# Reciprocal roots by logarithm and exponential, and a ring of four places for the block operands, in a one-core Hymba layer

## The chip, the cores and the metric

The kernel runs on one core of a Trainium2 chip. The metric is the device time in microseconds (us) of one execution. A core has five engines that run their own instruction queues in order: PE (TensorE: matrix products and transposes), DVE (VectorE), ACT (ScalarE: functions from loaded tables, copies with a scale), POOL (GpSimd, used here mostly to issue stores) and SP (SyncE, which issues loads). They meet through semaphores.

## The reference

One layer of a hybrid decoder on a prompt of 1024 tokens and on eight sequences of one new token each, model width 1024, all in fp32:

```python
hn = rmsnorm(x, g_norm)
u = hn @ w_in                                  # one input projection, 1024 x 7176
xa, za, uq, uk, uv, uo, zb, ui, uf = jnp.split(u, SPLIT_IDX, axis=-1)
yA = rglru_branch(xa, ...)                     # conv of 4, gates, linear recurrence
h, C, n, m = mlstm_seq(q, k, v, ig, lf, ...)   # 4 heads of 256, chunks of 128 tokens
yB = jax.nn.sigmoid(uo) * hB
yB = yB * lax.rsqrt(jnp.mean(yB * yB, axis=-1, keepdims=True) + EPS)   # one norm per token and head
merged = concat[yA * silu(za), yB * g_mhead * silu(zb)]
x = x + merged @ w_out                         # 2048 -> 1024
y = x * lax.rsqrt(jnp.mean(x * x, axis=-1, keepdims=True) + EPS) * g_final
```

It returns y for the prompt and for the new tokens, and the states of both branches.

## The kernel before

Every fp32 product is made of three matmuls on operands that are split into a rounded high part (a copy by ACT, `split`, L72) and the remainder (a subtraction by DVE, L73); in the groups of the profile they are L66, L67 and L68 of `mm3`. Large products are done in blocks by a scheme with seven products instead of eight.

The first 650 us or so make the input projection, the RG-LRU branch and the decode step of the mLSTM. What the change touches lies behind that. There the loop over n = 4..31 goes through 8 chunks of 128 tokens and, in each, 4 heads. For each n it emits the work of one head: `m_k` (weights `We` by an exponential on ACT, the split of q into `qh`, `ql` and of the state into `Ch`, `Cl`), `m_a` (scores in `ps_s`, keys `kh`, `kl`, weighted scores `ph`, `pl`, values `vh`, `vl`), `m_b` (products with the state in `ps_qp`, keys by values in `ps_kv`, scores by values in `ps_tr`, the new state `Cf`, the head's output `hh`) and `m_g` (gate by `so`, sum of squares by a Square on ACT). At the start of the next chunk `m_n` takes the reciprocal root for the four heads of the chunk before, a tile `ms` of 128x4; `m_zg` multiplies the four `hh` by it on ACT, and `m_z` transposes them on PE (into `ps_s` for the first two heads, `ps_qp` for the others) and multiplies by `z`. The root is `rsqrt`: a Sqrt on ACT, a reciprocal on DVE, a correction in one step (128x1) or two (128x4), and another reciprocal. The function needs a table, which ACT loads by an instruction of its own (ACT_TABLE_LOAD); where Sqrt follows an exponential or the reverse, a load stands ahead of it.

Between these pieces `fill` puts pieces of the output projection. For the first two thirds they are the 28 products `r_prod` of the seven-product scheme, over blocks whose operands `r_op` splits from raw blocks in DRAM (`d_ro`). The raw blocks come through a ring of SBUF places: two tiles of four (`ring0`, `ring1`), so that `r_op(n)` fetches block n + 8 into the place it has just split. `ring1` takes a slot (number 5) that an earlier weight operand held, and is opened in `r_prod(1)`; the same slot later holds z's block `zb0`, which is read back from DRAM. After the products come `out_part` pieces for the rows of tokens that go through the plain scheme, tile by tile (`wo` with `mh`, `ml`), each ending in an add on DVE (`y`, L1562) and a Square on ACT (L1563), and in `finish`, which takes a reciprocal root of a 128x1 tile `fms` and scales y for its store. `last_tile` does the same for the last 128 tokens with its own root (a tile `ms` of 128x1), and ends the kernel with two scalings (`yg`, L1593 on DVE and L1594 on ACT) and two stores.

The code emits instructions in this order; a scheduler in the framework then sets the order of each engine's queue, except where a stretch is put in by hand for PE. So another function or another count of operations can also move what stands around it.

Of the kernel before, what the change touches and what calls it, by code (L numbers as in the profile page):

```python
# [9 lines left out]
F32 = mybir.dt.float32  # L10
F32R = mybir.dt.float32r
BF16 = mybir.dt.bfloat16
AF = mybir.ActivationFunctionType
ALU = mybir.AluOpType
# [3 lines left out]
P = 128  # L18
T = 1024
HT = 512  # L20
# [31 lines left out]
def hymba_kernel(  # L52
# [7 lines left out]
    V, A, G, TE = nc.vector, nc.scalar, nc.gpsimd, nc.tensor  # L60
# [28 lines left out]
    rawp = ctx.enter_context(tc.tile_pool(name="rawp", bufs=1))  # L89
# [96 lines left out]
    def rsqrt_mean(out, v, t, n):  # L186

        V.tensor_scalar(v, v, 0.25 / n, 0.25 * EPS, op0=ALU.mult, op1=ALU.add)
        rsqrt(out, v, t)

    def rsqrt(out, v, t):

        A.activation(out, v, AF.Sqrt)
        V.reciprocal(t, out)
        if len(v.shape) == 2 and v.shape[1] == 1:
            V.scalar_tensor_tensor(t, v, t, out, op0=ALU.mult, op1=ALU.add)
        else:
            V.tensor_tensor(t, t, v, op=ALU.mult)
            V.tensor_tensor(t, t, out, op=ALU.add)
        V.reciprocal(out, t)  # L200
# [36 lines left out]
    def dec_unit(u):  # L237

        pz = ps("tr", [P, 512])
        for k in range(KC):  # L240
            g = k % 4
            TE.matmul(pz[32 * g:32 * g + 32, :], hnd[:, NB * k:NB * k + 32], raws[u, k // 4][:, k % 4, :], start=k < 4, stop=k >= 4,  # L242
                      skip_group_check=True)
        Z = sg([P, 512], "Z")
        A.copy(Z, pz)

        def turn():
            pt = ps("tr", [P, 4, P])
            for m in range(4):
                TE.transpose(pt[:, m, :], Z[:, m * P:(m + 1) * P], idF)  # L250
            for a, (kind, j) in enumerate(units[u]):
                src = pt[:, 2 * a:2 * a + 2].rearrange("p m (g b) -> p m b g", g=4)[:, :, 0:NB, :]
                V.tensor_reduce(dec_dst[kind](j), src, axis=mybir.AxisListType.X, op=ALU.add)
                if kind == "k":
                    V.tensor_scalar(dec_dst[kind](j), dec_dst[kind](j), 1.0 / 16.0, None, op0=ALU.mult)
        late.append(turn)
# [4 lines left out]
    def blk(u, a, b):  # L261
        return raws[u, b][:, :, a * 256:(a + 1) * 256]

    def prep(u, q):
        if q == Q_P5:
            dec_unit(u)
            V.tensor_tensor(blk(u, 0, 0), blk(u, 0, 0), blk(u, 1, 0), op=ALU.subtract)
            V.tensor_tensor(blk(u, 1, 0), blk(u, 1, 0), blk(u, 1, 1), op=ALU.add)
        if q == Q_P6:
            V.tensor_tensor(blk(u, 1, 0), blk(u, 1, 1), blk(u, 0, 0), op=ALU.subtract)  # L270
        src = {Q_P1: (0, 0), Q_P2: (0, 1), Q_P5: (1, 0), Q_P6: (1, 0), Q_P7: (0, 0), Q_P3: (0, 1), Q_P4: (1, 1)}
        hi, lo = ws([P, 4, 256], f"wh{u}_{q}"), ws([P, 4, 256], f"wl{u}_{q}")
        split(hi, lo, blk(u, *src[q]))
        wops[u, q] = hi, lo
        if q == Q_P6:
            V.tensor_tensor(blk(u, 0, 1), blk(u, 0, 1), blk(u, 1, 0), op=ALU.subtract)
        b = {Q_P7: 0, Q_P4: 1}.get(q)
        if b is not None:
            if u + 1 < len(units):
                load_raw(u + 1, b)  # L280
            else:
                if b == 1:
                    r_open(0)

    px = {}

# [976 lines left out]
    def m_n(c):  # L1263

        m = ch[c]["m"]
        dn, ss, t, rs, u = (m[:, n] for n in range(5))
        V.scalar_tensor_tensor(t, dn, -1.0, em_t[:, c, :], op0=ALU.mult, op1=ALU.max)
        V.tensor_tensor(t, t, dn, op=ALU.max)
        V.scalar_tensor_tensor(t, t, 0.25 * EPS, t, op0=ALU.mult, op1=ALU.mult)
        V.scalar_tensor_tensor(t, ss, 0.25 / (4 * 256), t, op0=ALU.mult, op1=ALU.add)  # L1270
        rsqrt(rs, t, u)

    def m_zg(c):

# [54 lines left out]
    def slot(n, name, dt=F32R):  # L1329
        if n < 0:  # L1330
            return rawp.tile([P, 4, HT], dt, tag="raw0", name=name)
        return big(n, [P, 4, HT], name, dt)
# [53 lines left out]
    rring = []  # L1386
    rops = {}
    rx = {}

    def r_open(n):  # L1390

        rring.append(rawp.tile([P, 4, HT], F32, tag="raw1", name="ring0") if n == 0 else slot(5, "ring1", F32))
        for i in range(4):
            r_fetch(4 * n + i)

    def r_slot(n):
        return rring[n % 8 // 4][:, n % 4, :]

    def r_fetch(n):

        if n < NR:
            p, q = n // 7, RQ[n % 7]
            ld(r_slot(n), d_ro[q][:, p].rearrange("p k t -> p (k t)"))

    def r_op(n):

        if n < NR:
            rops[n] = o = ws([P, 2, HT], f"ro{n}")
            split(o[:, 0], o[:, 1], r_slot(n))
            r_fetch(n + 8)  # L1410

    def put(c, a, t):
        stq(d_p[c][a], t, accum_op=ALU.add)
# [1 line left out]
    def r_prod(n):  # L1415

        p, q = n // 7, RQ[n % 7]
        if n < 2:
            w_step((Q_P4, Q_P3)[n])
        if n == 1:  # L1420
            r_open(1)
        r_op(n + 2)
        o = rops.pop(n)
        oh, ol = (o[:, i].rearrange("p (k t) -> p k t", k=4) for i in range(2))
        wh, wl = wr[q]
        if q == Q_P1:
            rx["X"] = ps("o", [P, 512])
        if q in (Q_P2, Q_P5):
            rx["Y"] = ps("o", [P, 512])
        X, Y = rx["X"], rx.get("Y")  # L1430
        out = X if q in (Q_P1, Q_P6, Q_P7, Q_P4) else Y
        for k in range(4):
            mm3(out, oh[:, k, :], ol[:, k, :], wh[:, k, :], wl[:, k, :], q in (Q_P1, Q_P2, Q_P5) and k == 0,
                q in (Q_P2, Q_P4, Q_P3) and k == 3)
            if k % 2:
                yield
        c = 4 * (p // 2) + p % 2
        if q in (Q_P1, Q_P5, Q_P6, Q_P4):
            rx[q] = t = sg([P, HT], f"r{q}")
            A.copy(t, Y if q == Q_P5 else X)  # L1440
            if q == Q_P4:
                put(c, 1, t)
        else:
            t = rx.pop({Q_P2: Q_P1, Q_P7: Q_P5, Q_P3: Q_P6}[q])
            V.tensor_tensor(t, t, X if q == Q_P7 else Y, op=ALU.add)
            put(c if q == Q_P2 else c + 2, q == Q_P7, t)
        r_after(n - (NR - 7))
# [59 lines left out]
    def finish(n, yt, ms, dst, later=False):  # L1507

        V.tensor_scalar(ms[:n, 0:1], ms[:n, 0:1], ms[:n, 1:2], 0.25 / T, op0=ALU.add, op1=ALU.mult)
        V.tensor_scalar(ms[:n, 0:1], ms[:n, 0:1], 0.25 * EPS, None, op0=ALU.add)  # L1510
        rsqrt(ms[:n, 2:3], ms[:n, 0:1], ms[:n, 3:4])

        def out():
            for half in range(2):
                hs = slice(half * HT, (half + 1) * HT)
                V.scalar_tensor_tensor(yt[half][:n], yt[half][:n], ms[:n, 2:3], mx["gf"][half][:n], op0=ALU.mult, op1=ALU.mult)
                stq(dst[:, hs], yt[half][:n])
        if later:
            tails.append(out)
        else:  # L1520
            out()
# [49 lines left out]
    def last_tile():  # L1571
        ms = mx["p2"].tile([P, 6], F32, tag="ms7", name="ms7")
        y = [sg([P, HT], f"y{n}") for n in range(2)]
        yg = [sg([P, HT], f"yg{n}") for n in range(2)]
        for n in range(2):
            ld(y[n], d_p[NCH - 1][n])
        mh, ml = ch[NCH - 1]["mh"], ch[NCH - 1]["ml"]
        for i, cs in enumerate(LP):
            p = ps("o", [P, 512])[:, 0:cs.stop - cs.start]
            for k in range(8):  # L1580
                w = wo[8 + k]
                mm3(p, mh[:, k, :], ml[:, k, :], w[:, 0, cs], w[:, 1, cs], k == 0, k == 7)
            v = (y[0], y[1][:, 0:256], y[1][:, 256:512])[i]
            vg = (yg[0], yg[1][:, 0:256], yg[1][:, 256:512])[i]
            gv = (mx["gf"][0], mx["gf"][1][:, 0:256], mx["gf"][1][:, 256:512])[i]
            V.tensor_tensor(v, v, p, op=ALU.add)
            A.activation(p, v, AF.Square, accum_out=ms[:, i:i + 1])
            V.tensor_tensor(vg, v, gv, op=ALU.mult)
            if i == 1:
                V.tensor_scalar(ms[:, 0:1], ms[:, 0:1], ms[:, 1:2], T * EPS, op0=ALU.add, op1=ALU.add)  # L1590
        V.tensor_scalar(ms[:, 0:1], ms[:, 0:1], ms[:, 2:3], 0.25 / T, op0=ALU.add, op1=ALU.mult)
        rsqrt(ms[:, 4:5], ms[:, 0:1], ms[:, 5:6])
        V.tensor_scalar(yg[0], yg[0], ms[:, 4:5], None, op0=ALU.mult)  # L1593
        A.mul(yg[1], yg[1], ms[:, 4:5])  # L1594
        for n in range(2):
            ld(y_p[0, (NCH - 1) * P:T, n * HT:(n + 1) * HT], yg[n])
# [152 lines left out]
    while work:  # L1749
        fill(1)  # L1750
    tail()
    last_tile()
    es_m.close()

# [32 lines left out]
```

## Time and profile before

| | us |
|---|---|
| time, median of 3 runs | 923.3 |
| lowest, highest | 921.3, 925.6 |
| the profiled execution | 925.6 |
| its span | 923.8 |
| PE busy | 905.8 (98%) |
| DVE busy | 742.0 (80%) |
| ACT busy | 613.6 (66%) |
| POOL busy | 192.7 (21%) |

A line of the timeline gives the start in us from the span's start, the duration, the engine, the line of the kernel, the operation, what it writes and reads by the names of the program, and in brackets the idle time ahead of it with what ended it. A line of waits gives total, times and longest. A line of a group gives busy time and the mean of one instruction in ns. Some 1.8 us of the execution lie outside of its span.

### The profile page before, as it was taken

The numbers are of one execution on the slowest core, as the hardware profiler recorded it, in microseconds if no ns is written. First come the engines' busy times: TensorE is split into PE (matmuls) and PEld (weight loads), VectorE is DVE, ScalarE is ACT, GpSimd is POOL, SyncE is SP. The second block draws the span as 40 slices with busy tenths as digits, with TensorE's granted clock in tenths as the row PEclk, the third lists the DMA queues.
The fourth block names the chain that finished last, engine by engine and source line by source line (L and its number), as shares of the span: only waits on it lengthen the run. The fifth ranks groups of instructions, "written<-read, shape, count | busy, mean of one in ns | idle before, by whom it ended". The sixth has DMA issues, their size and how long they took to land.

```text
span 923.8 us, 15540 instructions
## 1 busy us (share of the span) xinstructions
PE 905.8 (98%) x5261; PEld 749.8 (81%) x5261; DVE 742.0 (80%) x1535; ACT 613.6 (66%) x1088; POOL 192.7 (21%) x317
## 2 busy tenths in 40 slices
PE   8999999999999999999999999999999999999997
PEld 6798777777787988787789898877778888878886
DVE  6776778978688878789888876679997779888874
ACT  7654446866667776576758775446878579687772
POOL 1111113112312222324332324010111111110120
PEclk9999999999999999999999999999999999999999
DMA  6611457365746566547665647336588879755753
GB/s 195 212 46 40 143 151 251 127 207 176 239 141 205 171 202 195 187 145 260 210 232 168 252 137 241 107 131 220 181 241 242 212 209 294 189 163 149 197 106 94
DMA packets 130600, 167.87 MB, mean 182 GB/s; under 512 B 17620, under 2 KB 98580, under 8 KB 130514
## 3 DMA queue, kind: packets, MB, share of 16 engines
q1 hardware_dynamic: 108938, 103.94, 37.4%
q0 software_dynamic: 21584, 62.95, 20.7%
q8 instruction: 41, 0.67, 0.3%
q14 instruction: 37, 0.30, 0.1%
HBM read 108.19 MB, written 62.92 MB: 185 GB/s over the span
## 4 chain that ended last, share of the span: by engine, by line
PE 82%; DMA 6%; ACT 4%; DVE 4%; issue 2%; SPq 0%; POOL 0%; ACTq 0%; DVEq 0%; POOLq 0%
PE ps_o L66 14%; PE ps_o L68 13%; PE ps_o L67 13%; PE ps_kv L66 10%; PE ps_kv L67 9%; PE ps_kv L68 9%; PE ps_tr L242 2%; DMA Cb<-in_state_mlstm_C_dram 2%; PE ps_s L1181 1%; PE ps_qp L67 1%; DMA x<-in_x_prompt_dram 1%; PE ps_qp L68 1%; PE ps_qp L66 1%; PE ps_qp L999 1%; PE ps_tr L250 1%
## 5 line engine op out<-in xcount | busy, mean ns | idle before, releaser
L72 ACT CAST wh<-raw 128x1024 fp32r<-128x1024 f32 x91 | 95.4, 1049 | 76.3 <-PE ps_o L67 24.3
L73 DVE TENSOR_TENSOR wl<-raw,wh 128x1024 fp32r<-128x1024 f32 x91 | 111.1, 1220 | 31.2 <-ACT wh L72 17.9
L66 PE MATMUL ps_kv<-cb_hi,wh 128*128 128x512 f32 x320 | 127.5, 398 | 0.0
L68 PE MATMUL ps_kv<-cb_hi,wl 128*128 128x512 f32 x320 | 125.3, 392 | 0.0
L67 PE MATMUL ps_kv<-cb_lo,wh 128*128 128x512 f32 x320 | 125.2, 391 | 0.0
L66 PE MATMUL ps_o<-cb_hi,wh 128*128 128x512 f32 x240 | 94.6, 394 | 0.0
L68 PE MATMUL ps_o<-cb_hi,wl 128*128 128x512 f32 x240 | 93.6, 390 | 0.0
L67 PE MATMUL ps_o<-cb_lo,wh 128*128 128x512 f32 x240 | 93.5, 390 | 0.0
L66 PEld LDWEIGHTS ps_kv<-cb_hi,wh 128*128 128x128 f32 x320 | 60.1, 188 | 21.4 <-issue 4.6
L67 PEld LDWEIGHTS ps_kv<-cb_lo,wh 128*128 128x128 f32 x320 | 60.2, 188 | 13.4 <-issue 1.7
L68 PEld LDWEIGHTS ps_kv<-cb_hi,wl 128*128 128x128 f32 x320 | 60.1, 188 | 12.9
L66 PE MATMUL ps_kv<-wh,cb_hi 128*128 128x256 f32 x192 | 55.3, 288 | 0.3 <-ACT s L326 0.3
L67 PE MATMUL ps_kv<-wl,cb_hi 128*128 128x256 f32 x192 | 54.4, 283 | 0.0
L68 PE MATMUL ps_kv<-wh,cb_lo 128*128 128x256 f32 x192 | 54.3, 283 | 0.0
L66 PE MATMUL ps_o<-wo,mh 128*128 128x512 f32 (+1 forms) x136 | 53.2, 391 | 0.0
L66 PEld LDWEIGHTS ps_o<-cb_hi,wh 128*128 128x128 f32 x240 | 45.1, 188 | 9.9 <-issue 0.8
L68 PEld LDWEIGHTS ps_o<-cb_hi,wl 128*128 128x128 f32 x240 | 45.1, 188 | 9.8
L67 PEld LDWEIGHTS ps_o<-cb_lo,wh 128*128 128x128 f32 x240 | 45.1, 188 | 9.1
L68 PE MATMUL ps_o<-wo,ml 128*128 128x512 f32 (+1 forms) x136 | 51.8, 381 | 0.0
L67 PE MATMUL ps_o<-wo,mh 128*128 128x512 f32 (+1 forms) x136 | 51.4, 378 | 0.0
L66 PE MATMUL ps_o<-wh,cb_hi 128*128 128x256 f32 x144 | 40.9, 284 | 0.0
L67 PE MATMUL ps_o<-wl,cb_hi 128*128 128x256 f32 x144 | 40.7, 283 | 0.0
(545 smaller groups left out, 2624.5 us busy)
## 6 DMA issues: line engine op xcount, KB each, us to landing
raw<-in_w_in_dram SPq DMA_DIRECT2D x55, 512.0 KB
Cb<-in_state_mlstm_C_dram SPq DMA_DIRECT2D x32, 256.0 KB
out_dram<-Cb POOLq DMA_DIRECT2D x32, 256.0 KB, 4.4
qk<-d_qk SPq DMA_DIRECT2D x32, 256.0 KB
ring<-d_ro SPq DMA_DIRECT2D x28, 256.0 KB
d_qk<-s POOLq DMA_DIRECT2D x24, 256.0 KB, 4.4
d_x<-s POOLq DMA_DIRECT2D x16, 256.0 KB, 3.2
zsr<-d_y SPq DMA_DIRECT2D x16, 256.0 KB
```

The costliest lines, as they stand in the source:

```text
L66: TE.matmul(out, ah, bh, start=first, stop=False, skip_group_check=True)
L67: TE.matmul(out, ah, bl, start=False, stop=False, skip_group_check=True)
L68: TE.matmul(out, al, bh, start=False, stop=last, skip_group_check=True)
L72: A.copy(hi, src)
L73: V.tensor_tensor(lo, src, hi.bitcast(F32), op=ALU.subtract)
L242: TE.matmul(pz[32 * g:32 * g + 32, :], hnd[:, NB * k:NB * k + 32], raws[u, k // 4][:, k % 4, :], start=k < 4, stop=k >= 4, skip_group_chec ...
L250: TE.transpose(pt[:, m, :], Z[:, m * P:(m + 1) * P], idF)
L999: TE.matmul(pq[32 * g:32 * g + n, 0:256], q, ds_["C", h * NB + bb][:, kb, :], start=b == 1, stop=b == NB - 1, skip_group_check=True)
L1181: TE.matmul(S, qk[:, 2 + kb, :], qk[:, kb, :], start=kb == 0, stop=kb == 1)
```

## The change

A new function takes the reciprocal root as exp(-ln(v) / 2), with one Newton step on DVE. It replaces `rsqrt` in `m_n` (8 times, 128x4), in `finish` (8 times, 128x1 and once 8x1) and in `last_tile` (once, 128x1). The norm of the input, and other roots earlier, keep `rsqrt`. And the raw blocks' ring has one tile of four places; `r_op(n)` fetches block n + 4 into the place it has split, `ring1` is gone, and slot 5 goes straight to `zb0`. From the new function on, the lines stand 12 further down (10 from `r_prod` on).

```diff
+    def rsqrt_log(out, v, t):
+
+        A.activation(t, v, AF.Ln)
+        A.activation(out, t, AF.Exp, scale=-0.5)
+        if len(v.shape) == 2 and v.shape[1] == 1:
+            V.scalar_tensor_tensor(t, out, out, v, op0=ALU.mult, op1=ALU.mult)
+        else:
+            V.tensor_tensor(t, out, out, op=ALU.mult)
+            V.tensor_tensor(t, t, v, op=ALU.mult)
+        V.tensor_scalar(t, t, -0.25, 0.75, op0=ALU.mult, op1=ALU.add)
+        V.tensor_tensor(out, out, t, op=ALU.mult)
...
                 if b == 1:
-                    r_open(0)
+                    r_open()
...
     def m_n(c):
...
-        rsqrt(rs, t, u)
+        rsqrt_log(rs, t, u)
...
-    def r_open(n):
-
-        rring.append(rawp.tile([P, 4, HT], F32, tag="raw1", name="ring0") if n == 0 else slot(5, "ring1", F32))
+    def r_open():
+
+        rring.append(rawp.tile([P, 4, HT], F32, tag="raw1", name="ring"))
         for i in range(4):
-            r_fetch(4 * n + i)
+            r_fetch(i)
 
     def r_slot(n):
-        return rring[n % 8 // 4][:, n % 4, :]
+        return rring[0][:, n % 4, :]
...
             split(o[:, 0], o[:, 1], r_slot(n))
-            r_fetch(n + 8)
+            r_fetch(n + 4)
...
     def r_prod(n):
...
-        if n == 1:
-            r_open(1)
...
     def finish(n, yt, ms, dst, later=False):
...
-        rsqrt(ms[:n, 2:3], ms[:n, 0:1], ms[:n, 3:4])
+        rsqrt_log(ms[:n, 2:3], ms[:n, 0:1], ms[:n, 3:4])
...
     def last_tile():
...
-        rsqrt(ms[:, 4:5], ms[:, 0:1], ms[:, 5:6])
+        rsqrt_log(ms[:, 4:5], ms[:, 0:1], ms[:, 5:6])
```

In the built programs ACT has 61 table loads before and 70 now. Three places of the order, first ACT around `m_n(5)`, from the root's load to the gate of the next head. Before:

```order
L193 ACT_TABLE_LOAD
L193 ACTIVATE ms<-ms 128x4
L72 COPY qh<-qk 128x256
L72 COPY Ch<-Cf_5975 128x516
L1237 ACTIVATE hh<-ps_qp,gi_t 128x257
L193 ACTIVATE fms<-fms 128x1
L1189 ACTIVATE kh<-ps_s,de_t 128x256
L72 COPY vh<-vt 128x256
L193 ACTIVATE fms<-fms 8x1
L1277 ACTIVATE hh<-hh,ms 128x256
L72 COPY ph<-pf 128x128
L1277 ACTIVATE hh<-hh,ms 128x256 x3
```

Now, ahead of which stand a first load, the Ln of `ms` and the Ln of the decode step's 8x1 `fms` (L193):

```order
L194 ACT_TABLE_LOAD
L194 ACTIVATE ms<-ms 128x4
L194 ACTIVATE fms<-fms 8x1
L72 COPY qh<-qk 128x256
L72 COPY Ch<-Cf_5975 128x516
L1249 ACTIVATE hh<-ps_qp,gi_t 128x257
L1573 ACTIVATE ps_o,fms<-y_9122 128x512
L72 COPY vh<-vt 128x256
```

and directly behind these:

```order
L1289 ACTIVATE hh<-hh,ms 128x256 x3
L1201 ACTIVATE kh<-ps_s,de_t 128x256
L193 ACT_TABLE_LOAD
L193 ACTIVATE fms<-fms 128x1
L1272 ACTIVATE so,ms<-hh 128x256
L194 ACT_TABLE_LOAD
L194 ACTIVATE fms<-fms 128x1
L72 COPY ph<-pf 128x128
L1289 ACTIVATE hh<-hh,ms 128x256
```

`kh` moved from the third place behind the state's copy to behind a Square and three `hh`, and `ph` behind two more loads and the gate's Square.

The second place is ACT around `m_n(6)`. Before, from the load for `We`:

```order
L1162 ACT_TABLE_LOAD
L1162 ACTIVATE We<-We 128x128
L193 ACT_TABLE_LOAD
L193 ACTIVATE ms<-ms 128x4
L72 COPY qh<-qk 128x256
L72 COPY Ch<-Cf_5975 128x516
L1563 ACTIVATE ps_o,fms<-y_9629 128x512
L1237 ACTIVATE hh<-ps_qp,gi_t 128x257
L1189 ACTIVATE kh<-ps_s,de_t 128x256
```

Now:

```order
L1174 ACTIVATE We<-We 128x128
L1573 ACTIVATE ps_o,fms<-y_9640 128x512
L193 ACT_TABLE_LOAD
L193 ACTIVATE ms<-ms 128x4
L72 COPY qh<-qk 128x256
L194 ACT_TABLE_LOAD
L194 ACTIVATE ms<-ms 128x4
L72 COPY Ch<-Cf_5975 128x516
L1249 ACTIVATE hh<-ps_qp,gi_t 128x257
L72 COPY vh<-vt 128x256
L1289 ACTIVATE hh<-hh,ms 128x256 x2
L1201 ACTIVATE kh<-ps_s,de_t 128x256
```

`We` has lost its load, the Exp's load stands ahead of `Ch`, and two `hh` ahead of `kh`. On PE the transposes of `hh` into `ps_s` moved ahead of the `Ch` products of this piece.

The third place is the end of the loop, the root of the last chunk and of one output tile. ACT before:

```order
L1563 ACTIVATE ps_o,fms<-y_9870 128x512
L193 ACT_TABLE_LOAD
L193 ACTIVATE ms<-ms 128x4
L193 ACTIVATE fms<-fms 128x1
L1277 ACTIVATE hh<-hh,ms 128x256 x4
```

ACT now:

```order
L1573 ACTIVATE ps_o,fms<-y_9882 128x512
L193 ACT_TABLE_LOAD
L193 ACTIVATE ms<-ms 128x4
L194 ACT_TABLE_LOAD
L194 ACTIVATE ms<-ms 128x4
L193 ACT_TABLE_LOAD
L193 ACTIVATE fms<-fms 128x1
L194 ACT_TABLE_LOAD
L194 ACTIVATE fms<-fms 128x1
L1289 ACTIVATE hh<-hh,ms 128x256 x4
```

Four loads stand ahead of the four `hh` where one did. On PE the four transposes of `hh` into `ps_s` stand two matmuls further ahead. In what follows, the next output tile's `fms` and the last tile's `ms` have two loads each, where before they had none.

## Prediction

> **What bounds the kernel now.** I read the page first, then the waits of PE in the second half, then the instructions at each place where a root is taken. The page's busy row and the chain that ended last:
>
> ```profile
> PE 905.8 (98%) x5261; PEld 749.8 (81%) x5261; DVE 742.0 (80%) x1535; ACT 613.6 (66%) x1088; POOL 192.7 (21%) x317
> ...
> PE 82%; DMA 6%; ACT 4%; DVE 4%; issue 2%; SPq 0%; POOL 0%; ACTq 0%; DVEq 0%; POOLq 0%
> ```
>
> PE is the bound, and it stands still hardly at all. Its waits from 600 us to the end, of which three lines matter here:
>
> ```profile
> PE ps_qp L1286 <- ACT hh L1237: 1.2, 1, 1.2
> ...
> PE ps_s L1286 <- ACT hh L1277: 0.7, 1, 0.7
> PE ps_o L66 <- ACT ro L72: 0.4, 1, 0.4
> ```
>
> So a PE that runs full has next to nothing to win: what the change can give is in these lines, and what it can cost is every microsecond by which an operand now comes after PE asks for it. The roots are ACT's. The line of the root (the tile `ms` of m_n and of the last tile), with the loads of ScalarE's tables (min/median/max in ns), and the loads ahead of We's exponential:
>
> ```profile
> L193 ACT ACT_TABLE_LOAD  x13: 1283/1283/1283, 631.5 to 895.3; - x13
> L193 ACT ACTIVATE ms<-ms x9: 203/206/208, 632.8 to 918.5; 128x4 f32<-128x4 f32 x8, 128x1 f32<-128x1 f32 x1
> ...
> L1162 ACT ACT_TABLE_LOAD x11 | 14.1, 1283 | 0.2
> ```
>
> A load is 1.28 us and the root 0.2 us: the load is the price.
>
> **The change: arithmetic.** On DVE each root keeps its count: reciprocal, one or two steps, reciprocal become three or four steps of the same sizes, so the work there costs nothing. What changes is ACT. In the order of the changed program every Ln has a load ahead of it, and every Exp as well. In the stretch of m_n the second load replaces the one ahead of We, so their number stays, but both now stand ahead of the root's consumers, and what is queued behind them on ACT (qh, Ch, hh, kh, ph) is what PE asks for. I price the places one after another.
>
> **The last tile.** The end of before on ACT, and DVE's step ahead of the root:
>
> ```profile
> 917.99 0.19 ACT L1587 ACTIVATION_READ_ACCUMULATOR ps_o<-y 128x1 f32 x1
> 918.46 0.20 ACT L193 ACTIVATE ms<-ms 128x1 f32<-128x1 f32 x1 [0.28 <-DVE ms L1591]
> 919.35 0.72 ACT L1594 ACTIVATE yg<-yg,ms 128x512 f32<-128x512 f32 x1 [0.68 <-DVE ms L200]
> ...
> 918.21 0.21 DVE L1591 TENSOR_SCALAR ms<-ms 128x1 f32<-128x1 f32 x1 [0.18 <-ACT ps_o L1587]
> ```
>
> No load is left here before. Now the Ln's load starts at 918.18, when the accumulator is read, and hides only DVE's step: Ln 919.47 to 919.67, the Exp's load to 920.95, Exp to 921.15, against a root that ended at 918.66. DVE's steps behind it keep their 0.69 (918.66 to 919.35). This is the chain that ends the kernel: **+2.5**.
>
> **m_n of the last chunk.** ACT, then PE:
>
> ```profile
> 895.10 0.19 ACT L1563 ACTIVATION_READ_ACCUMULATOR ps_o<-y 128x1 f32 x1
> 895.31 1.28 ACT L193 ACT_TABLE_LOAD   x1
> 896.60 0.21 ACT L193 ACTIVATE ms<-ms 128x4 f32<-128x4 f32 x1
> 897.67 1.71 ACT L1277 ACTIVATE hh<-hh,ms 128x256 f32<-128x256 f32 x4 [0.77 <-DVE ms L200]
> ...
> 896.95 0.39 PE L66 MATMUL ps_o<-wo,mh 128*128 128x512 f32 x1
> 897.17 0.39 PE L67 MATMUL ps_o<-wo,mh 128*128 128x512 f32 x1
> 898.24 0.84 PE L1286 MATMUL ps_s<-idF,hh 128*128 128x128 f32 x4 [0.68 <-ACT hh L1277]
> ```
>
> Before: one load, two roots, hh at 897.67, and PE already waits 0.68 for it. Now four loads (5.13) and four functions (0.8) stand ahead of hh: 895.31 + 5.93 = 901.24, 3.57 later, with DVE's steps for ms done under the second pair. PE also meets the transposes two matmuls earlier (2 x 0.22), with nothing else to run: **+4.0**, between 3.6 and 4.4. These rows also answer what a switch costs here: the load starts 0.02 after the accumulator's end and the root starts 0.01 after the load's end. [...]
>
> **m_n(5), the sixth chunk's root.** ACT, then DVE's t and pl, then PE's first use of ph and of pl:
>
> ```profile
> 838.76 0.29 ACT L1162 ACTIVATE We<-We 128x128 f32<-128x128 f32 x1
> 839.72 0.60 ACT L1563 ACTIVATE ps_o<-y 128x512 f32<-128x512 f32 x1 [0.67 <-DVE y L1562]
> 840.46 1.28 ACT L193 ACT_TABLE_LOAD   x1
> 841.87 0.39 ACT L72 CAST qh<-qk 128x256 fp32r<-128x256 f32 x1
> 843.90 0.49 ACT L1277 ACTIVATE hh<-hh,ms 128x256 f32<-128x256 f32 x1
> 844.30 0.28 ACT L72 CAST ph<-pf 128x128 fp32r<-128x128 f32 x1
> 844.49 1.31 ACT L1277 ACTIVATE hh<-hh,ms 128x256 f32<-128x256 f32 x3
> 845.72 0.42 ACT L1260 ACTIVATE so<-hh 128x256 f32<-128x256 f32 x1
> 846.25 1.28 ACT L1162 ACT_TABLE_LOAD   x1
> ...
> 845.01 0.28 DVE L73 TENSOR_TENSOR pl<-pf,ph 128x128 fp32r<-128x128 f32 x1
> ...
> 847.30 0.28 PE L66 MATMUL ps_tr<-vh,ph 128*128 128x258 f32 x1
> 847.54 0.28 PE L68 MATMUL ps_tr<-vh,pl 128*128 128x258 f32 x1
> ```
>
> Now ph comes behind all of this, counted from We's end at 839.05: four loads 5.13; six small functions, some overlapped, 1.0; qh, Ch, hh, kh, vh 1.8 (841.87 to 843.90 less two roots); the Square 0.74 (839.72 to 840.46); three hh 1.23 (844.49 to 845.72); so 0.53 (845.72 to 846.25). That is 10.4: ph starts at 849.5, and pl ends 1.0 behind that start (844.30 to 845.29), at 850.5. PE asked at 847.54: **+3.0**. If DVE, which takes its queue in order, also stands behind each Exp with its Newton steps ahead of kl and pl, it is 5.
>
> **m_n(6).** DVE before, and PE's first product of that piece:
>
> ```profile
> 868.41 0.68 DVE L1562 TENSOR_TENSOR y<-y,ps_o 128x512 f32<-128x512 f32 x1
> 872.63 0.18 DVE L200 RECIPROCAL ms<-ms 128x4 f32<-128x4 f32 x1
> 872.72 0.67 DVE L73 TENSOR_TENSOR Cl<-Cf,Ch 128x516 fp32r<-128x516 f32 x1
> ...
> 874.15 0.28 PE L66 MATMUL ps_qp<-Ch,qh 128*128 128x258 f32 x1
> ```
>
> Square from 869.09 to 869.8, load 871.1, Ln and qh 871.65, load 872.95, Exp 873.1. The four Newton steps (about 1.0, as the root's steps before) now have Cl (0.67) and a sum of Cf between them: factor ready about 875.1, two hh (0.41 each) by 876.0. PE's order has the transposes of hh ahead of the Ch product now, at 874.15: **+2.0**; 3 if kh, behind the two hh on ACT, is late as well.
>
> **The other places.** Five m_n (chunks 0 to 4) keep their two loads, one of them earlier: each 0 to 1.5 (a load and its function, all late), nearest the low end since PE runs ring products there too and has work between the stages: 0.4 each, **+2.0**. Three pairs of fms in the m stretch get one more load ahead of PE's operands: 0 to 1.5, 0.5 each, **+1.5**. The pair at 907 lies in ACT's idle time of 4 us and costs nothing; with that gap gone, the next y would be 1 us late, still before the last tile's.
>
> **The ring.** The two rows where it shows before:
>
> ```profile
> 676.96 5.42 DMA ring<-d_ro
> ...
> 682.39 0.62 ACT L72 CAST ro<-ring 128x512 fp32r<-128x512 f32 x1 [1.71 <-DMA ring<-d_ro]
> ```
>
> The second ring opens late, its first loads land after 5.42, ACT waits 1.71 for one, and PE the 1.2 and 0.4 of its waits. With one ring places 4 and up are fetched as the splits go, and these waits can go: a gain of at most 1.6. Against it a place is refilled only four products ahead; a transfer of 5.4 against the four products of about 3 us fits, but if one is late the whole of ACT's queue waits behind the copy: up to 4 slower. I take **-1.0**. Loads on SP keep their number; zb0's move ahead and wait for a store at most some us with the same ring loads behind, in that range.
>
> **Sum**: 2.5 + 4.0 + 3.0 + 2.0 + 2.0 + 1.5 - 1.0 = +14.0 on the profiled execution's 925.6 (span 923.8 and 1.8 around it), 939.6; that execution is the slowest of three and 2.3 over the median, so **937.3**.
>
> **Rivals.** (1) Absorbed: the scheduler's order leaves enough cover in the middle, and only the end pays, 2.5 + 4.0: about 929.8. For it: PE has other products between the stages; against it: PE waited hardly at all before, so ACT and DVE were just in time only because of the order that has now moved. (2) DVE stands behind each Exp: 5 and 3 at m_n(5) and (6), 1.5 at two m_n and 1.5 at each fms pair: 4.0 + 2.5 + 8 + 3 + 1.2 + 4.5 - 1.0 = 22, about 945.5. For it: each Newton step is queued ahead of kl or pl. (3) The ring starves: ACT waits at several splits, 4 instead of -1.0 and some 3 more at splits that follow: 945. For it: the 1.71 at eight ahead; against it: before, it came from the late opening, not from the depth. (4) Not slower: one table holds logarithm and exponential. Then the loads of L193 and L1162 vanish from the m stretch, the last m_n starts hh 1.28 less 0.4 earlier (0.7 of it counts), the last tile pays 0.2 for the second function and the ring gives 1.6: 921.2. It decides as soon as one load fewer per pair is issued; the program's order, with a load ahead of each Ln and each Exp, is against it. [...]
>
> **How the numbers follow.** 0.5% of 923.3 is 4.6 us, about what a measurement here can tell from no change: 918.7 to 927.9. My forecast (934 to 942) 0.55; absorbed 0.2, with a quarter of it under 927.9 if stalls go as well; DVE 0.12; ring 0.06; one table or no cost 0.07, of which 0.03 is faster. So faster 0.03, same 0.09, slower 0.88. The range takes in the absorbed and the DVE case: 928.5 to 946.
>
> **What would show it.** Right: 70 table loads; PE waits of about 4 at the last transposes of ps_s on hh, 3 at ps_tr on ph or pl near 847, 2 near 874; yg 2.5 later behind the last Square; the wait of ro on the ring gone. Wrong: PE's waits after 700 still about 1 in all (absorbed), ACT ro waiting on the ring several times (ring), or Exp without a load.

## The result: 41 us slower, and the profile after

The changed kernel takes 965.9 us (median of 4 runs, 965.6 to 966.5) against 924.5 for the kernel before in the same comparison: ratio 1.044, interval 1.041 to 1.047. The forecast was 937.3 in a range of 928.5 to 946. The direction was right, the size was a third of what came.

The page of the changed kernel, busy time and the chain that ended last:

```profile
PE 918.8 (95%) x5261; PEld 756.7 (79%) x5261; DVE 742.2 (77%) x1535; ACT 629.2 (65%) x1114; POOL 192.8 (20%) x317
...
PE 74%; ACT 7%; DVE 7%; DMA 6%; issue 4%; POOL 0%; SPq 0%; ACTq 0%; DVEq 0%; POOLq 0%
```

The span grew by 40.0 us (923.8 to 963.8), and two things on PE make it up: PE's idle time grew by 27 (18.0 to 45.0), and its busy time by 13.0 with the same 5261 matmuls. The same work took longer, and that needs a cause of its own. DVE's busy time is unchanged (742.0, 742.2).

PE's waits from 640 us on, the largest five (total, times, longest):

```profile
PE ps_s L1298 <- ACT hh L1289: 8.1, 2, 4.4
PE ps_o L66 <- ACT r L1450: 5.2, 2, 3.8
PE ps_tr L1474 <- DVE hh L1256: 4.6, 1, 4.6
PE ps_qp L1298 <- ACT hh L1249: 3.1, 3, 2.0
PE ps_qp L66 <- ACT ps_qp L1546: 2.0, 1, 2.0
```

With the smaller ones it is 28.5, against 3.1 before. How much later the same matmul starts in the changed kernel's trace is called PE's lag below: it is 0.2 until 672 us, 7.8 after m_n(1), 10.4 after m_n(2), 11.6 after m_n(3), 18.1 after m_n(4), 25.8 after m_n(5) with the fms pair ahead of it, 31.5 after m_n(6), 37.5 after the last m_n; the last tile adds 2.5 to the span. So every chunk from m_n(1) on pays, not only the last three.

The last m_n, ACT and the transposes on PE:

```profile
925.80 0.19 ACT L1573 ACTIVATION_READ_ACCUMULATOR ps_o<-y 128x1 f32 x1
926.01 1.28 ACT L193 ACT_TABLE_LOAD   x1
927.52 1.28 ACT L194 ACT_TABLE_LOAD   x1
929.04 1.28 ACT L193 ACT_TABLE_LOAD   x1
930.56 1.28 ACT L194 ACT_TABLE_LOAD   x1
932.41 1.71 ACT L1289 ACTIVATE hh<-hh,ms 128x256 f32<-128x256 f32 x4 [0.36 <-DVE ms L201]
...
932.97 1.12 PE L1298 MATMUL ps_s<-idF,hh 128*128 128x128 f32 x4 [4.39 <-ACT hh L1289]
```

From the first load to hh it is 6.40, against 2.36 before (895.31 to 897.67): 4.04 more, and PE waits 4.39 instead of 0.68. At m_n(6) PE waited for the third `hh`, which stands behind kh and the gate's Square on ACT:

```profile
903.59 0.49 ACT L1289 ACTIVATE hh<-hh,ms 128x256 f32<-128x256 f32 x1
...
904.15 0.96 PE L1298 MATMUL ps_s<-idF,hh 128*128 128x128 f32 x4 [3.72 <-ACT hh L1289]
```

The last tile, ACT:

```profile
955.46 0.19 ACT L1597 ACTIVATION_READ_ACCUMULATOR ps_o<-y 128x1 f32 x1
955.66 1.28 ACT L193 ACT_TABLE_LOAD   x1
957.17 1.28 ACT L194 ACT_TABLE_LOAD   x1
959.34 0.72 ACT L1604 ACTIVATE yg<-yg,ms 128x512 f32<-128x512 f32 x1 [0.67 <-DVE ms L201]
```

From the accumulator to yg 3.88, against 1.36 before (917.99 to 919.35): 2.52 more. No gap stands between a load and what follows it here either (926.01 + 1.28 + 0.20 is 927.49, and the next load starts at 927.52).

### The profile page after: what moved, and what is told of

Its sections match the earlier page's. It is cut to its first block, busy times and chain, and to the rows that moved or that the text cites. A ratio compares the mean times of both kernels' runs of the same rounds, so it can differ in the third digit from the quotient of the medians.

```text
span 963.8 us, 15553 instructions
## 1 busy us (share of the span) xinstructions
PE 918.8 (95%) x5261; PEld 756.7 (79%) x5261; DVE 742.2 (77%) x1535; ACT 629.2 (65%) x1114; POOL 192.8 (20%) x317
## 4 chain that ended last, share of the span: by engine, by line
PE 74%; ACT 7%; DVE 7%; DMA 6%; issue 4%; POOL 0%; SPq 0%; ACTq 0%; DVEq 0%; POOLq 0%
PE ps_o L66 12%; PE ps_o L68 11%; PE ps_o L67 11%; PE ps_kv L66 9%; PE ps_kv L67 9%; PE ps_kv L68 9%; PE ps_tr L254 2%; DMA ring<-d_ro 2%; ACT L193 1%; ACT L194 1%; DMA Cb<-in_state_mlstm_C_dram 1%; PE ps_qp L1011 1%; PE ps_s L1193 1%; PE ps_tr L262 1%; DMA x<-in_x_prompt_dram 1%
## 5 line engine op out<-in xcount | busy, mean ns | idle before, releaser
L66 PE MATMUL ps_o<-wo,mh 128*128 128x512 f32 (+1 forms) x136 | 54.4, 400 | 0.0
L67 PE MATMUL ps_o<-wo,mh 128*128 128x512 f32 (+1 forms) x136 | 52.6, 387 | 0.0
```

The lines of the kernel that those rows point to most:

```text
L66: TE.matmul(out, ah, bh, start=first, stop=False, skip_group_check=True)
L67: TE.matmul(out, ah, bl, start=False, stop=False, skip_group_check=True)
```

## Experiments

The first question was which of the two edits pays, and whether it is the loads.

**The ring alone** (`ring_only`): the change with `rsqrt` put back.

```diff
-        rsqrt_log(rs, t, u)
+        rsqrt(rs, t, u)
```

and the same in `finish` and `last_tile`.

> The ring of four places with the old roots (Sqrt and reciprocals). Theory 1, the roots' table loads carry the loss: within 2 us of the kernel before, 922 to 926, PE's waits of 1.2 on hh and 0.4 on ro near 680 changed and nothing else. Rival 2, the ring starves (the waits of PE on r and of ACT on the ring near 688 and 716): 930 to 940.

Measured: 931.6 against 923.5, ratio 1.009 (1.0067 to 1.0112), some 8 us slower. The waits of ACT from 640 to 770 us on the ring's loads, with a ring of four:

```profile
ACT ro L72 <- DMA ring<-d_ro: 9.2, 6, 4.0
```

The kernel before had 1.7 in one wait. The copies of ro stand in ACT's queue, and the operands behind them wait with them. PE's largest wait of this kernel, 3.06 on kh, came behind a copy that waited 3.45:

```profile
686.64 0.62 ACT L72 CAST ro<-ring 128x512 fp32r<-128x512 f32 x1 [3.45 <-DMA ring<-d_ro]
687.17 0.47 ACT L1189 ACTIVATE kh<-ps_s,de_t 128x256 fp32r<-128x256 f32 x1
...
687.69 0.80 PE L66 MATMUL ps_kv<-vh,kh 128*128 128x258 f32 x2 [3.06 <-ACT kh L1189]
```

So the rival holds, near the lower edge of its 930 to 940, and theory 1 is wrong on this edit. The wait of 3.45 begins on DVE. A block's place is read twice, by ACT's copy and by DVE's subtraction of the copy, and the refill is issued when the second is done. The copy of block 5, its subtraction and the load of block 9 into its place, of the same run:

```profile
667.70 0.63 ACT L72 CAST ro<-ring 128x512 fp32r<-128x512 f32 x1
...
680.70 0.68 DVE L73 TENSOR_TENSOR ro<-ring,ro 128x512 fp32r<-128x512 f32 x1
...
681.42 0.32 SPq L1403 DMA_DIRECT2D ring<-d_ro  x1
```

The subtraction ends 13.1 behind the copy (668.33, 681.38), the load is issued 0.04 later, and ACT, which reached its copy of block 9 at 683.19, starts it at 686.64. The wait of 4.0 has the same form: copy until 687.26, subtraction until 698.65, load at 698.70.

**The roots alone** (`log_all`): the kernel before with `rsqrt_log` at all 17 places and the ring of eight.

> The new roots at all 17 places with the old ring of eight places. Theory 1: nearly the whole loss, 961 to 967, with PE's waits on hh, r, and kh at each m_n. Rival 2, the ring starves: 10 us or more less than the changed kernel, 950 to 956, and the waits near 716 and 748 gone.

Measured: 960.3, ratio 1.039 (1.037 to 1.041), 36 us slower. It lies between the two expectations. PE's waits from 640 us on, four of them:

```profile
PE ps_s L1298 <- ACT hh L1289: 8.1, 2, 4.4
PE ps_tr L1476 <- DVE hh L1256: 4.6, 1, 4.6
PE ps_o L66 <- ACT r L1452: 2.4, 2, 1.4
PE ps_qp L66 <- ACT ps_qp L1548: 2.2, 2, 2.0
```

The roots carry most of the loss. Of the wait on r the 3.8 near 716 is gone: it needed both edits. With both, ACT at m_n(1) came 5 us late out of a wait on the ring, and then had two loads ahead of the copy that frees PE's accumulator (ACT rows, then PE, of the changed kernel):

```profile
706.47 0.62 ACT L72 CAST ro<-ring 128x512 fp32r<-128x512 f32 x1 [5.00 <-DMA ring<-d_ro]
...
711.01 1.28 ACT L193 ACT_TABLE_LOAD   x1
...
712.82 1.28 ACT L194 ACT_TABLE_LOAD   x1
...
715.92 0.58 ACT L1450 COPY r<-ps_o 128x512 f32<-128x512 f32 x1
...
716.55 0.80 PE L66 MATMUL ps_o<-wr4h,ro 128*128 128x512 f32 x1 [3.83 <-ACT r L1450]
```

**The loads away, the arithmetic kept** (`joint`, and `joint_ring8` with the ring of eight). One load of the set that holds both functions is put in by hand behind the second chunk's last gate; from there on, the program has no other.

```diff
-        A.activation(so, g, AF.Square, accum_out=x["m"][:, 1, h:h + 1])
+        sqs[n] = A.activation(so, g, AF.Square, accum_out=x["m"][:, 1, h:h + 1])
...
+        if c == 1:
+            with tc.issue_after(sqs[7].ins):
+                A.preload_act_table_set("natural_log_exp_and_others")
         rsqrt_log(rs, t, u)
```

> The changed kernel with one table load put in by hand behind the last gate of the second chunk, of the set that holds both Ln and Exp: 41 loads in the program instead of 70, none behind that point; the arithmetic and the Newton steps stay. Theory 1, the loads are the loss: all of it goes, 921 to 926, since from there on there are fewer loads than in the kernel before. Rival 3, the moved order and the Newton steps in DVE's queue are the loss: still 10 us or more above the kernel before, 935 to 955.

Measured: 932.8 against 923.5, ratio 1.010 (1.0075 to 1.013). Neither expectation was met: most of the loss goes, but not all, since I had expected nothing of the ring. What is left is as much as the ring costs alone (1.009). The next run takes the ring away too.

> The new roots with one load of the set that holds both Ln and Exp, put in behind the second chunk's last gate, and the old ring of eight places: 41 loads. Theory 1 with the ring's part as measured (the ring alone 8 us, the joint table with the ring 9): the time of the kernel before or a little less, 920 to 925, with PE's waits at the last chunk near or under the 0.7 of before. Rival 3, the Newton steps or the moved order have a price of their own: 927 or more.

Measured: 925.4 against 924.4, ratio 1.0013 (0.9994 to 1.0033): no difference from the kernel before. So at fixed arithmetic, the loads are worth about 36 - 1 = 35 us. The order stayed too: by the traces of `log_all` and of this kernel, 1033 of ACT's 1044 other instructions and 5254 of PE's 5261 match in order, so the moved order without the loads is not the loss. The logarithm, the exponential and the Newton steps by themselves cost nothing that can be told. This kernel has 1 load behind 640 us where the one before has 22, so a small price of theirs could be hidden by that; PE's waits before, 3.1 in all, bound it. ACT at the last m_n of this kernel, and all of PE's waits from 640 us on:

```profile
892.43 0.19 ACT L1579 ACTIVATION_READ_ACCUMULATOR ps_o<-y 128x1 f32 x1
892.52 0.19 ACT L193 ACTIVATE ms<-ms 128x4 f32<-128x4 f32 x1
892.74 0.21 ACT L194 ACTIVATE ms<-ms 128x4 f32<-128x4 f32 x1
893.08 0.20 ACT L193 ACTIVATE fms<-fms 128x1 f32<-128x1 f32 x1
893.32 0.20 ACT L194 ACTIVATE fms<-fms 128x1 f32<-128x1 f32 x1
893.88 1.71 ACT L1293 ACTIVATE hh<-hh,ms 128x256 f32<-128x256 f32 x4 [0.36 <-DVE ms L201]
...
PE ps_qp L1302 <- ACT hh L1250: 2.1, 1, 2.1
PE ps_kv L66 <- ACT kh L1202: 0.5, 1, 0.5
PE ps_o L66 <- ACT ro L72: 0.4, 1, 0.4
```

From the accumulator to hh it is 1.45, against 2.57 before with its one load, and PE does not wait for hh any more. PE's waits are 3.0 in sum all the same, against 3.1 before, for there is one new wait of 2.1, behind a load of y that DVE waited 5.57 for; why that load comes late was not tried. This kernel shows that one set serves both functions (no load stands between the Ln at 892.52 and the Exp at 892.74, and 1 load in all behind 640 us), and the changed kernel that the build does not choose it unasked: its own trace has 16 loads at L193 and 15 at L194.

**Each root's part** (`log_mn`, `log_finish`, `log_last`): the kernel before with the new root at one of its three places.

```diff
-        rsqrt(rs, t, u)
+        rsqrt_log(rs, t, u)
```

> The new root only in m_n (8 times), ring and the other roots as before: 65 loads. Theory 1, every root whose loads stand ahead of PE's operands costs a wait: the waits near 740, 782, 818, 866, 896 and 925 stay, those that hang on the decode step's and the tiles' roots (PE on ps_qp of the decode rows, 2.0) go: 943 to 952, and the finish roots carry the rest. Rival: the waits come from loads of the two kinds of root side by side on ACT, then this alone gives under 940.

Measured: 943.2, ratio 1.0198 (1.0178 to 1.0219), 18 us, at the lower edge of theory 1 and without the decode rows' wait.

> Only finish's eight roots are new (seven output tiles and the decode rows), ring and other roots as before: 67 loads. If the two kinds of roots only add up, the difference of the new roots at all places (36) and of m_n alone (19) and of the last tile (2.5): 14 to 16 more, 937 to 941, with PE's wait of 2.0 on the decode rows' copies. If the price is made where both kinds stand side by side on ACT (m_n(5), the last m_n), it is less than 10 more, under 934.

Measured: 938.2, ratio 1.0146 (1.0118 to 1.0173), 14 us, with the 2.0 on the decode rows' copies, as expected of roots that add up.

> Only the last tile's root is new, ring and all else as before. Theory 1: two loads on the chain that ends the kernel, one part of the first hidden by the step on DVE: 2.5 more, 925.5 to 926.5, and the last scaling of yg on ACT 2.5 after where it stood behind the last Square. Rival: the first load is hidden in the idle time of ACT ahead of the last Square, 1.2 more.

Measured: 926.7, ratio 1.0029 (1.0013 to 1.0044), 2.7 us, with 1.2 to 4.1 in the interval; the time alone does not exclude the rival's 1.2. This run's own rows do: from the accumulator (916.05) to yg (919.94) it is 3.89, 2.53 more than the 1.36 before.

The three sum to 34.5, the roots at all places cost 36. PE's waits of m_n alone, from 640 us on, the first four lines:

```profile
PE ps_s L1298 <- DVE kl L1203: 4.3, 3, 2.3
PE ps_tr L1476 <- DVE hh L1256: 2.7, 1, 2.7
PE ps_s L1298 <- ACT hh L1289: 2.4, 1, 2.4
PE ps_o L66 <- ACT r L1452: 2.4, 2, 1.4
```

Two of them end on DVE, though DVE has no more work than before. Its groups in the changed kernel, the first Newton step of each kind (mean, then idle time ahead of it and who ended it):

```profile
L196 DVE SCALAR_TENSOR_TENSOR fms<-fms 128x1 f32<-128x1 f32 (+1 forms) x8 | 1.7, 218 | 17.1 <-ACT fms L194 17.1
L198 DVE TENSOR_TENSOR ms<-ms 128x4 f32<-128x4 f32 x8 | 1.3, 162 | 17.5 <-ACT ms L194 17.5
```

DVE stood 34.6 us ahead of the 16 first steps. At m_n(4) both kinds come in a row: an fms step (idle 2.75) holds the step of m_n's own t behind it, so that m_n's two loads on ACT start only after the fms pair is through. At this place m_n's new root alone made PE wait 2.7 (the second line above), finish's alone 2.24 (`log_finish`, at 811.49), and both make it wait 4.65. DVE, then PE:

```profile
818.76 0.22 DVE L196 SCALAR_TENSOR_TENSOR fms<-fms 128x1 f32<-128x1 f32 x1 [2.75 <-ACT fms L194]
...
819.62 0.16 DVE L1282 SCALAR_TENSOR_TENSOR ms<-ms 128x4 f32<-128x4 f32 x1
...
823.05 0.16 DVE L198 TENSOR_TENSOR ms<-ms 128x4 f32<-128x4 f32 x1 [2.56 <-ACT ms L194]
...
825.89 0.42 DVE L1256 TENSOR_TENSOR hh<-ps_tr,hh 128x257 f32<-128x257 f32 x1
...
826.37 3.31 PE L1474 MATMUL ps_tr<-oraw,mAd 128*32 128x512 f32 x16 [4.65 <-DVE hh L1256]
```

**The depth of the ring** (`ring6`): the kernel before with two of the second tile's places used.

```diff
-        for i in range(4):
+        for i in range(4 - 2 * n):
             r_fetch(4 * n + i)
...
-        return rring[n % 8 // 4][:, n % 4, :]
+        i = n % 6
+        return rring[i // 4][:, i % 4, :]
...
-            r_fetch(n + 8)
+            r_fetch(n + 6)
```

> The kernel before with two of the second ring tile's four places used: a ring of six, refetched six products ahead, opened where it was. Theory 5, the depth is what the ring of four lacks (ACT waited 9.2 us in 6 waits on its loads there, 1.7 in 1 with eight): between the two, 925 to 929, ACT's waits on the ring 3 to 7 us. Rival, what costs in the ring of four is that loads of slot 5 (zb) and others moved in SP's queue: with slot 5 as before, 923 to 925 and at most one wait on the ring.

Measured: 927.2, ratio 1.003 (1.0011 to 1.0048), about 3 us, between eight places (0) and four (8), and ACT waits 2.7 in two on the ring. The time fits the depth; the waits are just under what I had put for it, and slot 5 stands as before, so the rival's reason is not needed. Some of its part in the ring of four is not excluded.

**The busy time** (`warm`, `warm7`). After the long waits the profile shows a lower clock granted to PE. Stretches of the changed kernel around two of them (PE busy and its count first, the granted clock behind POOL):

```profile
700.00:716.00 16.00, 11.86 (x69) 9.94 (x67) 9.42 (x30) 9.74 (x23) 0.84 (x1) 1.00 0.83 235
716.00:724.00 8.00, 7.45 (x35) 6.40 (x36) 5.73 (x17) 6.06 (x17) 1.42 (x2) 0.79 0.34 87
...
932.00:940.00 8.00, 7.03 (x24) 5.75 (x25) 5.24 (x11) 3.72 (x9) 1.12 (x2) 0.60 0.35 103
```

0.79 over 8 us is 3.4 us at half, 0.60 is 6.4. Inside such a stretch matmuls of 512 columns start 0.43 apart (718.00, 718.43), outside 0.23 (720.75, 720.98). To try whether this costs time, products whose result is not read fill the wait:

```diff
+        if pair == 0 and c >= 6:
+            dm = ps("tr", [P, 512])
+            for i in range(14):
+                w = wo[8 + i % 4]
+                TE.matmul(dm, w[:, 0, 0:128], w[:, 0, 0:512], start=True, stop=True, skip_group_check=True)
         ht = ps(("s", "qp")[pair], [P, 4, P])
```

> The changed kernel with 14 extra products of 512 columns (3.2 us, their result is not read) on PE just ahead of the transposes of the last two chunks, where PE waited 3.7 and 4.4. Theory 4, PE runs at half its clock for some us after a wait that long, which is part of the loss: the waits shrink to about 0.5 and 1.2, the granted clock stays at 1 there, and the time falls by 2.5 to 4, to 962 to 963.5. Rival: only the waits themselves cost; the products fill them and the time stays within 0.7 of the changed kernel's.

Measured: 970.5, ratio 1.049 (1.046 to 1.052), some 5 us slower than the changed kernel (1.041 to 1.047, so the intervals just overlap) and against both expectations. At m_n(6) the products themselves waited 1.96 for their accumulator, which DVE still read, and what came behind them then waited 3.28 on ACT: my edit made a new wait there. So the next run has it at the last m_n alone (`c == 7`).

> The changed kernel with the 14 extra products (3.2 us) ahead of the transposes of the last chunk alone. Theory 4, half the clock after the wait is part of the loss: from the matmuls ahead of that place to the last output tile PE falls behind by 2 to 2.5 less than in the changed kernel (6.05 there), the clock stays at 1, and the time is 963 to 964.5. Rival, only the wait costs: the same 6 us there and the same time.

Measured: 964.4, ratio 1.0435 (1.0412 to 1.0458); the time alone cannot be told from the changed kernel's. The place can. The stretch of the same times in this kernel:

```profile
932.00:940.00 8.00, 6.78 (x34) 5.25 (x33) 3.70 (x12) 6.47 (x11) 1.12 (x2) 1.00 0.59 109
```

ACT's four loads stand as before and hh comes as late, PE waits 1.22 for it instead of 4.39, the clock stays at 1, and by the same matmuls PE falls behind by 3.7 across the last m_n instead of 6.05. The 2.35 between them is the price of the low clock at this place. The profiled execution was not faster in sum, since other stretches of it ran at half clock where the changed kernel's profile had none (at 793 and 878 us, and one unit more at 827). It is the slowest of this kernel's four (967.4, the others 962.0 to 964.8), and whether the total gains the 2.35 is not shown.

## Why the prediction was wrong, point by point

- **What bounds it: right.** PE ran full, and whatever came after PE asked was paid for. That the loads are the price is shown by `joint_ring8`.
- **The last tile: right.** 2.5 forecast, 2.52 in the rows, 2.7 by itself.
- **The last m_n: mechanism right, size short.** 4.0 forecast; hh came 4.04 later and PE waited 3.71 more. But PE fell 6.05 behind, 2.3 of it in the matmuls after the wait.
- **m_n(5): the sum right, in part by luck.** 3.0 forecast, 3.5 by PE's lag. ACT's part was right: from We's end to ph 10.2 (860.18 to 870.40) against 10.4. But PE waited only 0.75 for ph, where the forecast had all of it, and 1.99 at the transposes into `ps_qp` (874.82). These hung on the next head's hh (L1249), behind a We for which ACT had waited 1.65 on DVE, and no term of the forecast had that.
- **m_n(6): short.** 2.0 forecast; the wait on hh was 3.7, and PE fell back 5.7. I had the chain right: from the Square's start to the end of two hh it took 6.8 (896.15 to 902.93) against 6.9. But the first transpose waited for the third hh, 1.16 later (904.09), and the Square itself, forecast for 869.09, came 27.1 later than that, 1.3 more than PE's lag of 25.75. The rest, 2.0, is in the matmuls behind the wait.
- **"The other places" is the step that failed.** Five m_n at 0.4 each and three fms pairs at 0.5, 3.5 in sum. By PE's lag m_n(1) to m_n(4) cost 6.7, 2.6, 1.2 and 6.5 in the changed kernel, and the fms pair ahead of m_n(5) 3.8: over 20. With the roots alone (`log_all`) the same five cost 0.9, 2.6, 2.9, 6.5 and 2.3, some 15; most of the difference lies at m_n(1), where the wait on the ring comes on top. I reasoned that the number of loads stays and only one moves ahead, and that "work between the stages" covers it. PE's own queue gave no such cover: it is taken in order, and PE stood when its next operand was late (28.5 of waits from 640 us on, 3.1 before). The bound of 1.5 a place (one load and its function) did not hold even for one kind of root: at m_n(4) PE waited 2.7 with m_n's new root alone and 2.24 with finish's alone. Where both kinds meet the waits nearly add (4.65), since the Newton step of one root holds DVE and the next root's operand is behind it; the rows show that at m_n(4), for the other places it is not shown. My rival 2 (DVE stands behind each Exp) was nearest to this; its 945.5 was short because it kept the 1.5 a place and the gain on the ring, and had no clock.
- **The ring: wrong in sign.** -1.0 forecast, 8 us slower alone. The step that failed is "5.4 against the four products of about 3 us fits". It takes the refill to start at ACT's copy, but the refill is issued only when DVE has subtracted, 13.1 and 11.4 later in the two longest waits of `ring_only`; what is left of the four products is then 1.8 ahead of ACT's next copy of that place (681.42 to 683.19) and 3.7 (698.70 to 702.38), less than a transfer of 5.4. In `ring6` the subtraction followed at once, and the wait of 2.5 came because ACT's copies stand close there: four from 680.32 to 683.15, and the fifth waits. The upper end of 4 was too low as well. It also does not simply add: at m_n(1) it turned a wait of 1.0 (roots alone) into 3.8, while in the whole 8 and 36 gave 41.
- **What was not in the sum at all: the clock.** The page of the kernel before has a row for it, and I did not ask what a wait of 4 us does to it. That row could not have told: its only low stretch (0.91 in the last 23 us) begins at 919.9, behind PE's last matmul (917.1). The waits grew by 25.4; PE's lag grew by 37.3. Ahead of PE's last matmul the trace has five stretches at half clock behind 640 us, 20.5 us together; half of that, 10, is nearly all of the difference. With the one of 3.4 near 252 us, half of them is 12, most of the 13.0 by which PE's busy time grew. By `warm7` this was shown at one place, for the others it is read from the trace.

The range missed since I took all unknown places from their low ends and had no term for what one wait does to the next and to the clock.

## What to carry to other kernels

Where PE is 98% busy and every engine runs its queue in order, a table load is not priced by its 1.28 us but by what stands behind it: 9 more loads in the program and others moved ahead cost 36 us, and the same arithmetic without them next to nothing. Count the function switches of the built program, ask for a set that serves all functions of a stretch before replacing a formula, and price a place where two such chains meet as their sum (2.7 and 2.24 alone, 4.65 together at m_n(4)). A depth of prefetch is judged from the moment when the last reader of a place is done with it, here a subtraction on DVE 11 to 13 us behind the copy on ACT, to the next use where uses stand closest, and not by the mean distance of the uses.

## What the runs showed of the hardware

In these traces the granted clock falls to half in units of 3.4 us (0.50 from 716.6 to 720.0 in the changed kernel, one unit, and from 931.6 to 938.4, two), and not only after the long waits. In the profiled runs each wait of PE over 3 us (3.06 to 4.65) had such a stretch, one or two units long. Shorter ones had it in some runs and not in others at the same place: 1.98 on the decode rows' copies with it in the changed kernel and without in `log_all`; a pair of waits of 1.0 and 0.4 with it in `log_all`, without in the changed kernel. A wait of 2.80 had none (`joint`, at 826.50). The same is seen early in the program, where the code of all these kernels is the same: near 252 us a wait of 2.14 in the changed kernel had such a stretch, and one of 2.03 in `log_finish` had none. What decides it for the shorter waits is not shown.
